# Joining the delta rule's 32-blocks on VectorE, a 64-column last level, and two z tiles moved behind the last heads

## The chip, the cores and the metric

One core of one Trainium2 chip runs one layer of a hybrid decoder block on 256 tokens. The metric is the device time of one execution in microseconds (us). The engines are called as the profile calls them: PE (TensorE, matmuls), PEld (its weight loads), DVE (VectorE), ACT (ScalarE), POOL (GpSimd), SP (SyncE, which only issues DMAs here). ACT and POOL issue DMAs too; such an issue is an instruction in that engine's own queue, between its arithmetic.

## The reference, cut to what matters

The block has two mixers, a Mamba-2 branch and a Gated DeltaNet branch (16 heads, chunks of 64 tokens), then a product-key FFN. The part that the change touches is the inverse in the delta rule:

```python
kk = jnp.einsum('bnhid,bnhjd->bnhij', k, k)
lmat = jnp.where(strict, kk * beta[..., :, None] * decay, 0.0)
t_inv = lax.linalg.triangular_solve(eye + lmat, jnp.broadcast_to(eye, lmat.shape),
                                    left_side=True, lower=True, unit_diagonal=True)
u = t_inv @ (v * beta[..., None])
w = t_inv @ (k * (beta * jnp.exp(gc))[..., None])
```

The kernel uses chunks of 128 tokens, two per head, so each head needs two inverses of unit triangular 128x128 matrices.

## The kernel before, in words

All weights stream from HBM. A **unit** is one weight tile of 512 KB: SP loads it (`raw`), ACT rounds it to its upper part (`whi`, L106), DVE subtracts to get the lower part (`wlo`, L107), and PE runs 12 products of 512 columns on it (L383 to L385, each about a quarter of a microsecond). There are three buffers for the split halves, so when PE starts unit u, ACT can start splitting unit u+2, and units u and u+1 are ready. `schedule()` gives the order of the weight tiles: `qkv` of a head, `gz` (a z gate for two heads), `br gdn j` (the output projection of heads 2j and 2j+1).

Everything else runs as background generators: `bg.step()` is called after every half unit and emits the next step of a generator into the engines' queues when a planner's clock (`Clock`) says that its inputs will be through. The clock takes 0.1 us for a DMA issue on ACT and 4.5 us until it has landed. Once emitted, each engine runs its queue strictly in order. Before `br gdn j` starts, `bg.drain` emits whatever its two heads still lack.

A head (`gdn_gen`) writes its 128x128 matrices `at` to DRAM (`am`, L582). ACT reads the 16 diagonal blocks of 16x16 back, one to a partition (`cu`, L509), POOL inverts them in 30 small steps (L514 to L518) and writes them into `ym` (L522). ACT loads that as `xx` (L590). Then three levels (L592 to L614) join the blocks to 32, 64 and 128 on PE: each has a pair of transposes (L595), a pair of matmuls with the masked or cut `at` (L603, L605) and a pair with the result (L612); ACT and DVE move the results. After that comes the head's chain: `u` (L618, L620), `st` (L629 to L632), `vp` (L637 to L639), the second `u` (L643, L645), `o` (L648 to L661), and `yh`, `yl` (L673 to L676), which the projection reads.

Of the kernel before, what the change touches and what calls it, by code (L numbers as in the profile page):

```python
# [8 lines left out]
F = mybir.dt.float32  # L9
# [3 lines left out]
AF = mybir.ActivationFunctionType  # L13
OP = mybir.AluOpType
# [163 lines left out]
class Background:  # L178
# [61 lines left out]
def block(ctx, tc, nc, I, out, dbg=None):  # L240
    cp = ctx.enter_context(tc.tile_pool(name="consts", bufs=1))
# [3 lines left out]
    dram = ctx.enter_context(tc.tile_pool(name="dram", bufs=1, space=DRAM))  # L245
    V, S, G, PE = nc.vector, nc.scalar, nc.gpsimd, nc.tensor
# [33 lines left out]
    def ps_tile():  # L280
        return psp.tile([128, 512], F, name="pst")
# [6 lines left out]
    cst = cp.tile([128, 5 * 128], F, name="cst")  # L288
# [25 lines left out]
    def tr(dst, src):  # L314
        PE.transpose(dst, src, ident)  # L315
# [170 lines left out]

    corners = [[dram.tile([2, 8, 2064], F, name=n + str(i)) for n in ("am", "ym")] for i in range(2)]

    def whole(m):
        return m.rearrange("c b e -> c (b e)")[:, :128 * 128].rearrange("c (p t) -> p c t", t=128)

    def diagonal(m, i):
        return m[i, :, :2048].rearrange("b (r t) -> b r t", t=128)[:, :, 0:16]

    def clear_corners():
        G.memset(accg[:, 0, :258], 0.0)
        for _, ym in corners:
# [5 lines left out]
    def corner_inverses(am, ym):  # L505

        u, y, tm = (mx.tile([16, 16, 16], F, name=n, bufs=1) for n in ("cu", "cy", "ct"))
        for i in range(2):
            S.dma_start(u[8 * i:8 * i + 8], diagonal(am, i))  # L509
        G.memset(y, 0.0)  # L510
        G.memset(y.rearrange("p a b -> p (a b)")[:, 0:256:17], 1.0)
        yield
        yield pool_free
        for k in range(15, 0, -1):  # L514
            n = 16 - k
            G.tensor_tensor(tm[:, :k, :n], u[:, :k, k:k + 1].to_broadcast([16, k, n]),  # L516
                            y[:, k:k + 1, k:].to_broadcast([16, k, n]), op=OP.mult)
            G.tensor_tensor(y[:, :k, k:], y[:, :k, k:], tm[:, :k, :n], op=OP.subtract)  # L518
            if k in (11, 6):
                yield pool_free  # L520
        for i in range(2):
            G.dma_start(diagonal(ym, i), y[8 * i:8 * i + 8])  # L522
        yield

    def gdn_gen(h, pt, zg, yref):
# [48 lines left out]
        def level(l):  # L574
            b = mx.tile([128, 2, 128], F, name="lev", bufs=3)
            G.tensor_tensor(b, at[:, :, 1, :], masks[:, l - 4:l - 3, :].to_broadcast([128, 2, 128]), op=OP.mult)
            return b

        yield
        live["dT"] -= 1  # L580
        am, ym = corners[h % 2]
        S.dma_start(whole(am), at[:, :, 1, :])  # L582
        yield
        yield lambda: not live["c"] and "at once"
        live["c"] += 1
        yield from corner_inverses(am, ym)
        live["c"] -= 1
        b = level(4)
        xx = mx.tile([128, 2, 2, 128], F, name="xx", bufs=3)
        S.dma_start(xx[:, :, 1, :], whole(ym))  # L590
        yield
        for l in range(4, 7):  # L592
            pm = ps_tile().rearrange("p (a c b) -> p a c b", c=2, a=2)
            for c in range(2):
                tr(pm[:, 0, c, :], xx[:, c, 1, :])  # L595
            S.activation(xx[:, :, 0, :], pm[:, 0], AF.Copy)
            yield
            pm = ps_tile()[:, :256].rearrange("p (c a) -> p c a", c=2)
            m = mx.tile([128, 2, 128], F, name="mm", bufs=3)
            p0 = 64 if l == 6 else 0  # L600
            for c in range(2):
                if l < 6:
                    PE.matmul(pm[:, c, :], b[:, c, :], xx[:, c, 0, :], start=True, stop=True)  # L603
                else:
                    PE.matmul(pm[64:, c, :], at[:64, c, 1, 64:], xx[:64, c, 0, :], start=True, stop=True)  # L605
            S.activation(m[p0:], pm[p0:], AF.Copy)
            if l < 5:
                b = level(l + 1)
            yield
            pb = ps_tile()[:, :256].rearrange("p (c b) -> p c b", c=2)  # L610
            for c in range(2):
                PE.matmul(pb[:, c, :], m[p0:, c, :], xx[p0:, c, 1, :], start=True, stop=True)  # L612
            V.tensor_tensor(xx[:, :, 1, :], xx[:, :, 1, :], pb, op=OP.subtract)
            yield  # L614
        yield lambda: live["u"] < 2
        live["u"] += 1
        pu = ps_tile()
# [45 lines left out]
        if h > 1 and ("gdn", h // 2 - 1) not in merged:  # L663
            yield lambda: ("gdn", h // 2 - 1) in merged
        if h < 2 and not yref:
            mx.tile([128, 32], F, name="pad", bufs=1)
# [124 lines left out]

    small_e = [None, 0, False]
    over, past = set(), set()
    live = {"dT": 0, "u": 0, "c": 0}
    gens, ys, bcT, bcE, gts = {}, {}, {}, {}, {}
    zgs = {("gdn", j): [] for j in range(NH // 2)}

# [78 lines left out]
    for o in order:  # L876
# [20 lines left out]
        if t == ("gz", 0):  # L897
            first.close()
            aux = T16.tile([128, 4, 2, 512], F, name="t16")
            mx = mix.enter_context(tc.tile_pool(name="gdn", bufs=2))  # L900
            masks = mx.tile([128, 3, 128], F, name="masks", bufs=1)
            S.dma_start(masks, I["cst"][:, 1152:].rearrange("p (a b) -> p a b", a=3))
            clear_corners()
        if t == "small":
            evac(ps, 352, raw0)
# [410 lines left out]
```

## Time and profile before

| what | value |
|---|---|
| median of 3 runs | 3427.9 us (3427.09 to 3428.37) |
| the profiled execution | 3427.03 us |
| its span, first to last instruction | 3425.2 us |
| PE busy in the span | 3397.8 us (99%) |
| DVE, ACT, POOL busy | 2233.3, 1755.0, 498.8 us |
| heads of the delta rule | about 50 to 945 us of the span |

The times of the steps come from the profiled execution, so sums are made against its 3427.03 us; the median of the runs is 0.9 us above it. In a timeline each row is the start, the duration and the instruction; PE's matmuls overlap, so what a group of them costs is read from the starts of the products before and behind it.

### The profile page before, as it was taken

What the parts mean: (1) busy time and instruction counts of PE and PEld (TensorE: products, weight loads), DVE (VectorE), ACT (ScalarE), POOL (GpSimd) and SP (SyncE); (2) the same over time, 40 slices, a digit from 0 to 9 for tenths busy, and PEclk for the clock granted to TensorE, in tenths of its full rate; (3) what the DMA queues carried; (4) which work ended last, traced back from release to release, by engine and by line L of the source; (5) the groups of instructions that cost most, each with busy time, mean ns of one, the idle gap of its engine ahead of it and who ended that gap; (6) DMA issues with size and microseconds to landing.
All of it is one profiled execution on the core that took longest, in us unless ns stands there. A gap on an engine that the chain in (4) does not pass through costs nothing.

```text
span 3425.2 us, 43886 instructions
## 1 busy us (share of the span) xinstructions
PE 3397.8 (99%) x16118; PEld 2795.7 (82%) x16118; DVE 2233.3 (65%) x3150; ACT 1755.0 (51%) x2356; POOL 498.8 (15%) x753
## 2 busy tenths in 40 slices
PE   9999999999999999999999999999999999999998
PEld 7888888888888888888888888888888788888886
DVE  6665666676577777777665888766664455555555
ACT  6556555555445454545445445566655444444444
POOL 0434333334200000000000000133230000000000
PEclk9999999999999999999999999999999999999999
DMA  7545555555565555556565566677776877777774
GB/s 258 182 156 158 155 167 157 164 166 156 167 198 177 186 183 186 183 173 200 184 217 191 174 210 210 203 239 231 231 230 223 267 244 241 238 242 244 241 231 162
DMA packets 248408, 687.07 MB, mean 201 GB/s; under 512 B 26736, under 2 KB 86720, under 8 KB 247936
## 3 DMA queue, kind: packets, MB, share of 16 engines
q1 hardware_dynamic: 164960, 594.03, 54.1%
q10 hardware_dynamic: 81824, 87.60, 7.6%
q0 software_dynamic: 1408, 2.64, 0.3%
q8 instruction: 126, 2.06, 0.2%
q14 instruction: 90, 0.74, 0.1%
HBM read 645.81 MB, written 38.36 MB: 200 GB/s over the span
## 4 chain that ended last, share of the span: by engine, by line
PE 96%; DVE 1%; ACT 1%; issue 1%; ACTq 0%; POOL 0%; DMA 0%; POOLq 0%; SPq 0%; DVEq 0%
PE acc L383 23%; PE acc L384 22%; PE acc L385 22%; PE acc L1177 3%; PE acc L1178 3%; PE acc L1183 3%; PE pst L1177 3%; PE pst L1178 3%; PE pst L1183 3%; PE pst L315 3%; PE pst L1104 1%; PE pst L737 1%; PE pst L612 1%; DVE wlo L107 1%; ACT whi L106 0%
## 5 line engine op out<-in xcount | busy, mean ns | idle before, releaser
L107 DVE TENSOR_TENSOR wlo<-raw,whi 128x1024 fp32r<-128x1024 f32 (+1 forms) x1129 | 1419.8, 1266 | 900.5 <-ACT whi L106 898.7
L106 ACT ACTIVATE whi<-raw 128x1024 fp32r<-128x1024 f32 (+1 forms) x1129 | 1184.9, 1052 | 909.6 <-PE acc L385 517.8
L383 PE MATMUL acc<-whi,t 128*128 128x512 f32 (+2 forms) x2848 | 1157.4, 406 | 8.1 <-ACT whi L106 8.1
L384 PE MATMUL acc<-wlo,t 128*128 128x512 f32 (+2 forms) x2848 | 1108.8, 389 | 2.5 <-DVE wlo L107 2.2
L385 PE MATMUL acc<-whi,t 128*128 128x512 f32 (+2 forms) x2848 | 1109.1, 389 | 0.0
L385 PEld LDWEIGHTS acc<-whi,t 128*128 128x128 f32 x2848 | 535.9, 188 | 114.4
L383 PEld LDWEIGHTS acc<-whi,t 128*128 128x128 f32 x2848 | 536.5, 188 | 112.2 <-ACT whi L106 8.6
L384 PEld LDWEIGHTS acc<-wlo,t 128*128 128x128 f32 x2848 | 537.4, 189 | 106.5 <-DVE wlo L107 6.7
L1087 POOL TENSOR_TENSOR b<-ob,gp 128x1024 f16<-128x1024 f16 x64 | 121.5, 1898 | 607.7 <-ACT whi L106 334.0
L383 PE MATMUL acc<-whi,yh 128*128 128x512 f32 x512 | 209.3, 409 | 0.0
L1178 PE MATMUL pst<-wlo,t 128*128 128x512 f32 x512 | 199.9, 391 | 2.1 <-DVE wlo L107 2.1
L384 PE MATMUL acc<-wlo,yh 128*128 128x512 f32 x512 | 200.1, 391 | 0.4 <-DVE wlo L107 0.4
L385 PE MATMUL acc<-whi,yl 128*128 128x512 f32 x512 | 200.0, 391 | 0.0
L1177 PE MATMUL pst<-whi,t 128*128 128x512 f32 x512 | 199.9, 390 | 0.0
L1177 PE MATMUL acc<-whi,t 128*128 128x512 f32 x512 | 199.2, 389 | 0.0
L1178 PE MATMUL acc<-wlo,t 128*128 128x512 f32 x512 | 199.2, 389 | 0.0
L458 DVE SCALAR_TENSOR_TENSOR t<-pst,cols,t 128x255 f32<-128x255 f32 x336 | 135.9, 474 | 33.8 <-ACT t L454 33.7
L1183 PE MATMUL pst<-whi,t 128*128 128x512 f32 x508 | 156.8, 390 | 0.0
L1183 PE MATMUL acc<-whi,t 128*128 128x512 f32 x508 | 156.4, 389 | 0.0
L516 POOL TENSOR_TENSOR ct<-cu,cy 16x15 f32<-16x15 f32 (+7 forms) x240 | 96.8, 403 | 194.4 <-DMA cu<-am 177.0
L1178 PEld LDWEIGHTS pst<-wlo,t 128*128 128x128 f32 x512 | 96.4, 188 | 22.4 <-DVE wlo L107 2.4
L384 PEld LDWEIGHTS acc<-wlo,yh 128*128 128x128 f32 x512 | 96.3, 188 | 21.3 <-DVE wlo L107 1.3
(273 smaller groups left out, 3286.8 us busy)
## 6 DMA issues: line engine op xcount, KB each, us to landing
raw<-w_in SPq DMA_DIRECT2D x408, 512.0 KB
raw<-u SPq DMA_DIRECT2D x256, 512.0 KB
raw<-v SPq DMA_DIRECT2D x256, 512.0 KB
raw<-w_gdn SPq DMA_DIRECT2D x64, 512.0 KB
raw<-w_ssm SPq DMA_DIRECT2D x64, 512.0 KB
raw<-w_out SPq DMA_DIRECT2D x32, 512.0 KB
raw<-w_q SPq DMA_DIRECT2D x32, 512.0 KB
hdr<-ht ACTq DMA_DIRECT2D x32, 512.0 KB
```

The lines of the kernel that those rows point to most:

```text
L106: self.nc.scalar.activation(hi[:, s], t[:, s], AF.Copy)
L107: self.nc.vector.tensor_tensor(lo[:, s], t[:, s], hi[:, s].bitcast(F), op=OP.subtract)
L315: PE.transpose(dst, src, ident)
L383: PE.matmul(o, xa, h_, start=k == 0, stop=False)
L384: PE.matmul(o, xa, l_, start=False, stop=False)
L385: PE.matmul(o, xb, h_, start=False, stop=k == nk - 1)
L458: V.scalar_tensor_tensor(dst[:, s:], src[:, :T - s], w[:, c, k:k + 1], dst[:, s:], op0=OP.mult, op1=OP.add)
L516: G.tensor_tensor(tm[:, :k, :n], u[:, :k, k:k + 1].to_broadcast([16, k, n]), y[:, k:k + 1, k:].to_broadcast([16, k, n]), op=OP.mult)
L1087: G.tensor_tensor(b2, ob[:, None, :, :].to_broadcast([128, 2, 4, 128]), gp[:, :, ts, None].to_broadcast([128, 2, 4, 128]), op=OP.mult)
L1177: PE.matmul(o_, a, hi[:, s], start=i2 == 0, stop=False)
L1178: PE.matmul(o_, a, lo[:, s], start=False, stop=False)
L1183: PE.matmul(acc[tb][2 * hv + n], b, hi[:, n * 512:(n + 1) * 512], start=False, stop=False)
```

## The change

Per head, the join from 16 to 32 leaves PE. POOL also writes the 16x16 inverses and their transposes to a new DRAM tile `yb`. When that is done, ACT issues 18 DMAs in one step: 8 loads of the blocks beside the diagonal, broadcast so that each of 128 partitions holds one block and one column (`cb`, 64-byte rows), 8 of the second inverse (`c1`) and 2 of a column of the first (`c2`). DVE then multiplies and sums twice (128x256 each), and ACT writes the 16x16 results into `ym` with 2 DMAs. The join to 64 stays on PE (now from the transposed blocks), and the join to 128 uses 64x64 transposes and matmuls of 64 rows and 64 columns. There are 12 PE instructions per head in place of 18, and 25 DMA issues on ACT in place of 5. The corner buffers go from 2 to 3, the planner's backlog from 2.5 to 3.0, and z tile 6 moves from behind `br gdn 3` to behind `br gdn 5`, next to z tile 7, so that `br gdn 4` and `br gdn 5` each come one tile earlier.

```diff
-        if j != 6:
-            o.append(("in", ("gz", min(j + 1, 7))))
+        o += [("in", ("gz", i)) for i in ((1,), (2,), (3,), (4,), (5,), (), (), (6, 7))[j]]
...
-    def __init__(self, clock, backlog=2.5):
+    def __init__(self, clock, backlog=3.0):
...
+    def beside(m, i, below):
+
+        rows = m[i].rearrange("b e -> (b e)").rearrange("(j f) -> j f", j=4)[:, 2048 * below:2048 * below + 2048]
+        o = 0 if below else 16
+        return rows.rearrange("j (r t) -> j r t", t=128)[:, :, o:o + 16]
...
+        G.tensor_copy(tm, y.rearrange("p a b -> p b a"))
+        G.dma_start(yb[0].rearrange("c b e -> (c b) e"), y.rearrange("p a b -> p (a b)"))
+        G.dma_start(yb[1].rearrange("c b e -> (c b) e"), tm.rearrange("p a b -> p (a b)"))
         for i in range(2):
-            G.dma_start(diagonal(ym, i), y[8 * i:8 * i + 8])
+            G.dma_start(diagonal(ym, i), tm[8 * i:8 * i + 8])
+        live["c"] -= 1
+        yield
+        yield lambda: not live["d"] and "at once"
+        live["d"] += 1
...
+        for i in range(2):
+            for j in range(4):
+                S.dma_start(bb[64 * i + 16 * j:64 * i + 16 * j + 16],
+                            beside(am, i, 0)[j:j + 1].to_broadcast([16, 16, 16]))
+        for i in range(2):
+            for j in range(4):
+                p = slice(64 * i + 16 * j, 64 * i + 16 * j + 16)
+                S.dma_start(y1[p], yb[0, i, 2 * j:2 * j + 1].to_broadcast([16, 256]))
+            S.dma_start(y2[64 * i:64 * i + 64, 0, :],
+                        yb[1, i].rearrange("(j b) (q r) -> j b q r", b=2, q=16)[:, 1])
+        yield
+        V.scalar_tensor_tensor(pr, bb, -1.0, y2[:, 0:1, :].to_broadcast([128, 16, 16]), op0=OP.mult, op1=OP.mult)
+        V.tensor_reduce(y2[:, 1, :], pr, axis=mybir.AxisListType.X, op=OP.add)
+        V.tensor_tensor(pr, y1, y2[:, 1:2, :].to_broadcast([128, 16, 16]), op=OP.mult)
+        V.tensor_reduce(y2[:, 2, :], pr, axis=mybir.AxisListType.X, op=OP.add)
+        live["d"] -= 1
+        yield
+        for i in range(2):
+            S.dma_start(beside(ym, i, 1), y2[64 * i:64 * i + 64, 2, :])
...
+        for c in range(2):
+            PE.matmul(pm[:, c, :], b[:, c, :], xx[:, c, 0, :], start=True, stop=True)
+        for c in range(2):
+            tr(pb[:, c, :], xx[:, c, 0, :])
...
+        lo, hi = slice(0, 64), slice(64, 128)
+        pm = ps_tile()[:, :128].rearrange("p (c a) -> p c a", c=2)
+        for c in range(2):
+            PE.transpose(pm[lo, c, :], xx[lo, c, 1, lo], ident[lo, lo])
+        S.activation(xx[lo, :, 0, lo], pm[lo], AF.Copy)
+        yield
+        pm = ps_tile()[:, :128].rearrange("p (c a) -> p c a", c=2)
+        for c in range(2):
+            PE.matmul(pm[hi, c, :], at[lo, c, 1, hi], xx[lo, c, 0, lo], start=True, stop=True)
...
+            PE.matmul(pb[lo, c, :], m[hi, c, lo], xx[hi, c, 1, hi], start=True, stop=True)
```

Two places show what moves. The first is ACT's queue in the fifth head's chain (`u`, `st`, `o`, second `u`), before:

```order
L620 ACTIVATE u_3457<-pst,cc 128x256
L535 DMA dT<-racs 128x256
L632 ACTIVATE st<-pst 128x256
L634 ACTIVATE junk,so<-pst 128x256
L790 ACTIVATE t_3478<-acc,r_111 128x512 x2
L106 ACTIVATE whi<-raw 128x1024
L640 ACTIVATE o<-pst,ecs 128x256
L546 ACTIVATE junk,w_3512<-pst 128x128 x4
```

In the changed kernel, the same head's chain with the next head's 18 loads in it (`cb`, `c_3770` and `c_3772` are the tiles they fill; lines are those of the changed kernel):

```order
L661 ACTIVATE u_3743<-pst,cc 128x256
L105 ACTIVATE whi<-raw 128x1024
L545 DMA cb<-am_143 16x16x16 x8
L550 DMA c_3770<-yb_145 16x256 x4
L551 DMA c_3772<-yb_145 64x1x16
L550 DMA c_3770<-yb_145 16x256 x4
L551 DMA c_3772<-yb_145 64x1x16
L607 ACTIVATE vp<-pst,nk 128x256 x2
L105 ACTIVATE whi<-raw 128x1024
L673 ACTIVATE st<-pst 128x256
```

The same burst from its eighth DMA on, with the semaphores that each waits for. ACT's and SP's DMAs signal eight semaphores in turn (DMAHW0 to DMAHW7), so each waits for the last DMA that had its own:

```order
L545 DMA cb<-am_143 16x16x16 [waits DMAHW7_49]
L550 DMA c_3770<-yb_145 16x256 [waits DMAHW0_49,DMASW7_49]
L550 DMA c_3770<-yb_145 16x256 [waits DMAHW1_49]
L550 DMA c_3770<-yb_145 16x256 [waits DMAHW2_49]
L550 DMA c_3770<-yb_145 16x256 [waits DMAHW3_49]
L551 DMA c_3772<-yb_145 64x1x16 [waits DMAHW4_49,DMASW0_49]
L550 DMA c_3770<-yb_145 16x256 [waits DMAHW5_49]
L550 DMA c_3770<-yb_145 16x256 [waits DMAHW6_49]
L550 DMA c_3770<-yb_145 16x256 [waits DMAHW7_49]
L550 DMA c_3770<-yb_145 16x256 [waits DMAHW0_49]
L551 DMA c_3772<-yb_145 64x1x16 [waits DMAHW1_49]
```

So between `u` and `st` ACT has 18 DMA issues where it had one. The second place is PE's queue where `br gdn 5` begins (its products read `yh`), before:

```order
L383 MATMUL acc<-whi,t_105 128x512
L384 MATMUL acc<-wlo,t_105 128x512
L385 MATMUL acc<-whi,t_106 128x512
L612 MATMUL pst<-xx,mm 128x128 x2
L383 MATMUL acc<-whi,yh 128x512
```

And now (L684 and L689 are the second `u` and `o` of head 11, L314 on `o` the transposes that `yh` is made from):

```order
L384 MATMUL acc<-whi,t_106 128x512
L604 MATMUL pst<-cT 128x256 x2
L684 MATMUL pst<-vp,xx 128x256
L689 MATMUL pst<-u_7296,at 128x256
L314 MATMUL pst<-cst,t_6991 128x128 x4
L314 MATMUL pst<-cst,o 128x128 x4
L382 MATMUL acc<-whi,yh 128x512
```

The end of head 11's chain, which ran among the products of the tile before, now stands directly ahead of the projection, with no products between its steps.

## Rows read from the trace of the kernel before

**Rows 1.** Page, part 1: busy us, share of span, instructions of each engine.

```profile
PE 3397.8 (99%) x16118; PEld 2795.7 (82%) x16118; DVE 2233.3 (65%) x3150; ACT 1755.0 (51%) x2356; POOL 498.8 (15%) x753
```

**Rows 2.** Windows: length, PE, PEld, DVE, ACT, POOL busy, PE's clock, DMA share, GB/s.

```profile
250.00:350.00 100.00, 99.66 (x484) 81.51 (x483) 60.62 (x100) 61.27 (x117) 45.81 (x94) 1.00 0.51 159
```

**Rows 3.** Timeline of PE, one head's levels: start, duration, instruction.

```profile
403.55 0.61 PE L612 MATMUL pst<-xx,mm 128*128 128x128 f32 x4
...
404.23 0.39 PE L384 MATMUL acc<-wlo,t 128*128 128x512 f32 x1
...
405.39 0.38 PE L315 MATMUL pst<-cst,xx 128*128 128x128 f32 x2
405.61 0.60 PE L315 MATMUL pst<-cst,t 128*128 128x128 f32 x4
...
407.20 0.40 PE L385 MATMUL acc<-whi,t 128*128 128x512 f32 x1
407.53 0.65 PE L605 MATMUL pst<-xx,at 64*64 64x128 f32 x4
...
408.44 0.40 PE L384 MATMUL acc<-wlo,t 128*128 128x512 f32 x1
...
409.39 0.39 PE L385 MATMUL acc<-whi,t 128*128 128x512 f32 x1
409.70 0.71 PE L612 MATMUL pst<-xx,mm 64*128 64x128 f32 x4
...
410.68 0.40 PE L384 MATMUL acc<-wlo,t 128*128 128x512 f32 x1
```

**Rows 4.** Timeline of PE in the Mamba-2 branch, matmuls of 64 columns.

```profile
1025.62 1.89 PE L737 MATMUL pst<-xdt,sc 128*128 128x64 f32 x16
```

**Rows 5.** DMA issues by tile: issue time min/median/max in ns; last, landing of POOL's.

```profile
L509 ACTq DMA_DIRECT2D cu<-am x32: 288/332/535, 111.6 to 863.0; - x32
L590 ACTq DMA_DIRECT2D xx<-ym x16: 371/387/388, 143.9 to 894.5; - x16
DMA to landing us min/median/max: 1.9/3.3/5.2
```

**Rows 6.** Timeline of ACT late in the FFN: four DMA issues in a row (ACTq).

```profile
2683.33 1.06 ACT L106 ACTIVATE whi<-raw 128x1024 fp32r<-128x1024 f32 x1 [1.66 <-PE acc L385]
...
2686.06 2.99 ACTq L1139 DMA_DIRECT2D m<-gdr  x2
2689.07 3.85 ACTq L1143 DMA_DIRECT2D p<-hdr  x2
2693.03 1.06 ACT L106 ACTIVATE whi<-raw 128x1024 fp32r<-128x1024 f32 x1 [6.29 <-DMA m<-gdr]
```

**Rows 7.** Timeline of PE over the same stretch.

```profile
2691.78 0.39 PE L384 MATMUL acc<-wlo,t 128*128 128x512 f32 x1
2692.01 0.40 PE L385 MATMUL acc<-whi,t 128*128 128x512 f32 x1
2694.14 0.51 PE L383 MATMUL acc<-whi,t 128*128 128x512 f32 x1 [1.73 <-ACT whi L106]
2695.40 0.79 PE L384 MATMUL acc<-wlo,t 128*128 128x512 f32 x1 [0.75 <-DVE wlo L107]
...
2698.54 0.39 PE L385 MATMUL acc<-whi,t 128*128 128x512 f32 x1
```

**Rows 8.** Windows, just behind that: columns as in rows 2.

```profile
2695.10:2698.50 3.40, 3.10 (x7) 2.48 (x8) 2.40 (x3) 1.96 (x3) 0.00 (x0) 0.50 1.07 385
```

**Rows 9.** Timeline of ACT at the last head's end: second u, then yh.

```profile
933.37 0.48 ACT L645 ACTIVATE u<-pst,cc 128x256 f32<-128x256 f32 x1
...
942.45 0.48 ACT L330 ACTIVATE yh<-pst,cols 128x256 fp32r<-128x256 f32 x1 [0.74 <-PE pst L315]
```

**Rows 10.** Groups by line: count, busy us, mean ns of one, idle us before.

```profile
L613 DVE TENSOR_TENSOR xx<-xx,pst 128x256 f32<-128x256 f32 x48 | 19.9, 415 | 14.7 <-PE pst L612 14.7
L576 POOL TENSOR_TENSOR lev<-at,masks 128x256 f32<-128x256 f32 x32 | 35.9, 1129 | 0.0
```

More of the change, by code (lines that the diff above doesn't have):

```diff
@@ L485, in input_tile @@
         return mx.tile([128, 2, 512], F, name="t4", bufs=NT4[0])
-    corners = [[dram.tile([2, 8, 2064], F, name=n + str(i)) for n in ("am", "ym")] for i in range(2)]
+    corners = [(dram.tile([2, 8, 2064], F, name="am%d" % i), dram.tile([2, 8, 2064], F, name="ym%d" % i),
+                dram.tile([2, 2, 8, 256], F, name="yb%d" % i)) for i in range(3)]
     def whole(m):
@@ L503, in pool_free, with corner_inverses @@
         return "at once" if bg.clock.t["Pool"] < bg.clock.t["PE"] + 2.0 else False
-    def corner_inverses(am, ym):
+    def corner_inverses(am, ym, yb):
+        yield lambda: not live["c"] and "at once"
+        live["c"] += 1
         u, y, tm = (mx.tile([16, 16, 16], F, name=n, bufs=1) for n in ("cu", "cy", "ct"))
@@ L520, in corner_inverses @@
                 yield pool_free
+        G.tensor_copy(tm, y.rearrange("p a b -> p b a"))
+        G.dma_start(yb[0].rearrange("c b e -> (c b) e"), y.rearrange("p a b -> p (a b)"))
+        G.dma_start(yb[1].rearrange("c b e -> (c b) e"), tm.rearrange("p a b -> p (a b)"))
         for i in range(2):
-            G.dma_start(diagonal(ym, i), y[8 * i:8 * i + 8])
+            G.dma_start(diagonal(ym, i), tm[8 * i:8 * i + 8])
[3 more added lines that the diff above has]
+        live["d"] += 1
+        bb, y1, pr = (mx.tile([128, 16, 16], F, name=n, bufs=1) for n in ("cb", "c1", "cp"))
+        y2 = mx.tile([128, 3, 16], F, name="c2", bufs=2)
+        for i in range(2):
[17 more added lines that the diff above has]
+            S.dma_start(beside(ym, i, 1), y2[64 * i:64 * i + 64, 2, :])
         yield
@@ L572, in gdn_gen @@
             V.tensor_scalar(at[:, c, 1, :], at[:, c, 1, :], cc[:, c:c + 1], None, op0=OP.mult)
[L574 to L577, printed above, removed]
         yield
         live["dT"] -= 1
-        am, ym = corners[h % 2]
+        am, ym, yb = corners[h % 3]
         S.dma_start(whole(am), at[:, :, 1, :])
         yield
-        yield lambda: not live["c"] and "at once"
@@ L585, in gdn_gen @@
[L585 to L588, printed above, removed]
+        yield from corner_inverses(am, ym, yb)
         xx = mx.tile([128, 2, 2, 128], F, name="xx", bufs=3)
-        S.dma_start(xx[:, :, 1, :], whole(ym))
+        S.dma_start(xx[:, :, 0, :], whole(ym))
+        b = mx.tile([128, 2, 128], F, name="lev", bufs=2)
+        G.tensor_tensor(b, at[:, :, 1, :], mask[:, None, :].to_broadcast([128, 2, 128]), op=OP.mult)
         yield
[L592 to L614, printed above, removed]
@@ new lines, in gdn_gen @@
+        pm = ps_tile()[:, :256].rearrange("p (c a) -> p c a", c=2)
+        pb = ps_tile()[:, :256].rearrange("p (c a) -> p c a", c=2)
+        for c in range(2):
+            PE.matmul(pm[:, c, :], b[:, c, :], xx[:, c, 0, :], start=True, stop=True)
+        for c in range(2):
+            tr(pb[:, c, :], xx[:, c, 0, :])
+        m = mx.tile([128, 2, 128], F, name="mm", bufs=3)
+        S.activation(m, pm, AF.Copy)
+        V.tensor_copy(xx[:, :, 1, :], pb)
+        yield
+        pb = ps_tile()[:, :256].rearrange("p (c b) -> p c b", c=2)
@@ new lines, in gdn_gen @@
+        for c in range(2):
+            PE.matmul(pb[:, c, :], m[:, c, :], xx[:, c, 1, :], start=True, stop=True)
+        V.tensor_tensor(xx[:, :, 1, :], xx[:, :, 1, :], pb, op=OP.subtract)
+        yield
+        lo, hi = slice(0, 64), slice(64, 128)
[3 more added lines that the diff above has]
+        S.activation(xx[lo, :, 0, lo], pm[lo], AF.Copy)
+        yield
+        pm = ps_tile()[:, :128].rearrange("p (c a) -> p c a", c=2)
@@ new lines, in gdn_gen @@
+        for c in range(2):
+            PE.matmul(pm[hi, c, :], at[lo, c, 1, hi], xx[lo, c, 0, lo], start=True, stop=True)
+        m = mx.tile([128, 2, 128], F, name="mm", bufs=3)
+        S.activation(m[hi, :, lo], pm[hi], AF.Copy)
+        yield
+        pb = ps_tile()[:, :128].rearrange("p (c b) -> p c b", c=2)
+        for c in range(2):
+            PE.matmul(pb[lo, c, :], m[hi, c, lo], xx[hi, c, 1, hi], start=True, stop=True)
+        V.tensor_tensor(xx[lo, :, 1, hi], xx[lo, :, 1, hi], pb[lo], op=OP.subtract)
@@ L615, in gdn_gen @@
+        yield
         yield lambda: live["u"] < 2
@@ L665, in gdn_gen @@
         if h < 2 and not yref:
-            mx.tile([128, 32], F, name="pad", bufs=1)
+            mx.tile([128, 64], F, name="pad", bufs=1)
         if not yref:
@@ L900, in block @@
             mx = mix.enter_context(tc.tile_pool(name="gdn", bufs=2))
-            masks = mx.tile([128, 3, 128], F, name="masks", bufs=1)
-            S.dma_start(masks, I["cst"][:, 1152:].rearrange("p (a b) -> p a b", a=3))
+            live["d"] = 0
+            mask = mx.tile([128, 128], F, name="mask", bufs=1)
+            S.dma_start(mask, I["cst"][:, 1280:1408])
             clear_corners()
```

4 lines of the change are left out of this document (2 added, 2 removed).

## The prediction

> **What bounds the kernel now.** I read the page's busy line first: PE is busy 3397.8 of 3425.2 us [rows 1], so the time is the sum of PE's own instructions plus every moment in which PE is made to wait. Then the windows, to see whether the heads' stage is different: in 250 to 350 us PE is busy 99.66 of 100 us while DVE has 60.62, ACT 61.27 and POOL 45.81 [rows 2]. So each matmul that leaves PE is a gain in full, and work added to the others is free on the mean. The mean hides one thing: ACT feeds PE a split weight tile every unit, and PE has only two units ready when it begins one. So I then looked for a place where ACT's queue holds something long, and found one in the FFN [rows 6 to 8].
>
> The sum is made against the profiled run's 3427.0 us (span 3425.2 and 1.8 around it); the median of the runs is 3427.9, so 0.9 is added at the end.
>
> **What leaves PE.** What a group costs is read from the starts around it, less 0.23 us for each undisturbed product (2691.78 to 2692.01) [rows 7]. A pair of transposes: 405.39 to 405.61, 0.22. A pair of full matmuls: 403.55 to 404.23 holds the pair and one product, 0.68 - 0.23 = 0.45. The 64-row pairs are dearer: 407.20 to 408.44 holds two products and the pair, 1.24 - 0.46 = 0.78, and 409.39 to 410.68 gives 0.83 [rows 3]. The join to 32 is 0.22 + 0.45 + 0.45 = 1.12 us a head and goes: 16 x 1.12 = 18. The join to 64 keeps its six.
>
> The join to 128 is 0.22 + 0.78 + 0.83 = 1.83 now; no row shows its new form (64 rows and 64 columns). Sixteen passes of 64 columns took 1.89, 0.118 each [rows 4], and a pass of 128 columns costs 0.45 / 4 = 0.11 [rows 3], so by the nearest row half the columns save nothing. If time did follow columns, each matmul pair would save 0.22. The transposes become a 64-row group: 0.22 if that costs nothing, 0.22 + 0.33 if it pays what a 64-row pair pays over a full one (0.78 - 0.45). So the level lies between 1.39 and 2.16, a gain of 7 to a loss of 5 us over 16 heads; I take 0, by rows 4. PE's own work falls by 18 us (13 to 25).
>
> The Trainium skill, TensorEngine Tiling (Array Packing), section Key Properties, says that changing the tiling mode drains TensorE; the trace's 0.33 us over a full pair agrees with that, and the rule speaks against the third 64-row group. By that rule alone the sum would be some 5 us worse than mine.
>
> **What DVE and POOL get.** DVE has four new operations of 128x256 and a copy, and loses one subtract and most of another: at 0.415 us each [rows 10] about 1.7 us a head net. POOL loses one mask product of 1.13 [rows 10] and gets a copy and two DMA issues, about as much. Both are covered by the 39 and 54 idle us in 100 [rows 2], so I cost them at nothing; were DVE's cover gone, 16 x 1.7 = 27 us. DVE's first new operation also waits for the last of the loads, and `wlo` is queued behind it. The planner puts it 6.5 us behind the burst's start, the loads land later (below), but PE and the `wlo` ahead of it are late by the same cause by then, so this wait lies under that one and is not added. The two issues into `ym` and the load of `xx` wait as `am`, `cu` and `xx` did before.
>
> **What ACT gets: 18 DMA issues in a row, 16 times.** ACT loses three short activations a head, but its queue now holds a burst of 18 issues. One takes 0.33 us (L509) to 0.39 (L590) [rows 5], so the burst lasts 6.0 to 7.0 us by issue alone. With eight semaphores the eighth waits for the landing of the first, each later one for one some seven or eight ahead of it, and three or four for SP's loads. Landings are 1.9 / 3.3 / 5.2 us (min/median/max) for POOL's DMAs, the nearest row [rows 5]. With 3.3 the eighth goes at 3.3 behind the first, the sixteenth at 6.3, the seventeenth at 7.0, and the burst ends at 7.7; with 1.9 it is bound by issue, 7.0; with 5.2 it ends at 11.5. I take 7.7. The planner books 18 x 0.1 = 1.8 us, so what it emits behind the burst comes some 6 us too early.
>
> Queued behind it on ACT are the next `whi`, the previous head's `st`, second `u` or `o`, and `vp`; DVE waits for that `whi`, and PE for both and for the second `u` (L648 before, L689 now). A walk through the burst that is emitted behind unit 106, with t = 0 where PE starts that unit: the activation ahead of the burst starts at 0, so the issues run from 0 to 7.7; then `whi` for unit 108 (1.06) to 8.8, then the second `u` (0.48) at 9.3. PE reaches the matmul that needs it after one unit (12 x 0.23 = 2.75), one pair (0.45) and half a unit (1.38): 4.6. PE waits 4.7 us. Where no such matmul is near, as behind unit 61, the next `whi` decides: the burst starts 1.2 behind the start of unit 60 and ends at 8.9, the write of `am` takes 0.39, `whi` ends at 10.4 and `wlo` 1.26 later (2694.14 to 2695.40 [rows 7]) at 11.6; PE has three units and a pair, 9.1, and waits 2.5. In the same way the 15 bursts that lie among products give 2.3 to 4.7, 3.8 on the mean; all move one for one with the burst's length.
>
> The trace of before has one such case. Four issues held ACT from 2686.06 to 2693.03, 6.9 us, 2.7 behind a `whi` [rows 6]. PE then waited 1.73 and 0.75 us, and the granted clock behind it was 0.50, the 1.2 GHz level, for 3.4 us [rows 8]. From 2692.01 to 2698.54 PE made nine starts, which are 2.07 us of products: that burst cost 4.5 us [rows 7]. I take 4.5 for each of the 15, between 2.1 (burst of 6.0, full clock) and 5.5 (7.7, and each wait followed by 3.4 us at the half clock, worth 1.7): 67 us.
>
> **The sixteenth burst and the moved z tile.** With z tile 6 gone from there, `br gdn 5` follows head 11's input sooner, and the drain ahead of it emits the burst, the second `u` and the rest of the chain with no product between. From second `u` to `yh` took 9.1 us at the last head [rows 9]. Ahead of the second `u` stand what is left of the burst (7.7 less the 1.1 that it began before the tile's end, 6.6), and four activations, two for `vp` and two that evacuate the next head's input: 1.9 at 0.48 each (256 columns, rows 9), at most 4.2 at 1.06 (1024 columns, rows 6). With 1.9 the chain ends at 17.6; the transposes of `o`, behind which PE goes on, come 0.7 ahead of `yh`. PE fills 2.7 of it with its own groups (by rows 3, a matmul of 256 columns counted as two of 128, 4 x 0.45, and eight transposes, 4 x 0.22): 14 us of waiting, 11 to 18. The tiles themselves only change places.
>
> **Sum.** 3427.0 - 18 + 67 + 14 = 3490, and 0.9 for the median: **3491 us**.
>
> **Rivals.** *The bursts are hidden.* PE's two ready units would cover them if a burst were no longer than 7.7 - 3.8 = 3.9 us, 0.22 for an issue; then only the 18 us remain: 3427.9 - 18 = 3410 (3403 to 3415), faster. For it: ACT is idle 39 of 100 us. Against it: no issue of the 48 in rows 5 is under 0.288, and the four in rows 6 did hold ACT. I give it 0.09. The Trainium skill, DMA: Bandwidth & Descriptors, section Issuing engines are not separate DMA queues, calls the time to initiate a DMA on the sequencer usually small relative to the DMA, and Anatomy of one DMA puts the sequencer's dispatch at some 50 ns; by that a burst would be an estimated 0.9 us and this rival would hold, but the rows show six times as much.
>
> *The change does its work and gives it back.* Bursts of 6.0 with early landings and clocks that stay full would cost 2.1 each at most; were half of them covered too, 15 x 1.0 + 11 - 25 is near nothing: 3428 (within 0.2%, which is about what a measurement of this kernel can tell from no change). 0.05.
>
> *Issue alone counts.* Bursts of 6.0 and full clock everywhere: -18 + 31 + 11: 3452 (3436 to 3465). 0.17.
>
> *Landings count.* 64-byte rows landing as late as 5.2 make bursts of 11.5 and waits of 7.6, 9.3 with the half clock: -18 + 139 + 18: 3567. 0.09. Forecast: 0.60, with 3465 to 3535 for itself.
>
> **How the numbers follow.** Faster 0.09, same 0.05, slower 0.86. The range leaves out the two cases below (0.14) and most of the last: 3436 to 3535.
>
> **What would show it.** Right: ACT idle before `whi` of 6 to 8 us sixteen times with ACTq rows of L545 to L551 beside it; PE waiting 2 to 5 us at L689 or at the first product of a unit, each followed by a stretch at 0.50; one wait of about 14 us ahead of `br gdn 5`; PE's busy time at full clock down by some 18. The 64-row groups' starts show the last level. Wrong: ACTq issues well under 0.3 us, or `whi` starting between them, or PE at 99% in the windows of the heads' stage as before.

## The result: 3548.5 us, 3.5% slower than before

The changed kernel takes 3548.5 us (median of 4 runs, 3547.3 to 3550.1) against 3427.6 for the kernel before on the same chip: a ratio of 1.035 (95% interval 1.034 to 1.037). The direction and the mechanism were forecast, the size was not: +121 us in place of +63, above the range's end of 3535.

The page of the changed kernel, part 1, answers to [rows 1]. PE is busy 96% of a span that is 121 us longer:

```profile
PE 3411.1 (96%) x15958; PEld 2795.7 (79%) x15958; DVE 2256.2 (64%) x3214; ACT 1731.9 (49%) x2308; POOL 524.3 (15%) x786
```

The window of [rows 2], now: PE loses 12 of 100 us, and its mean clock falls to 0.93.

```profile
250.00:350.00 100.00, 87.26 (x395) 70.17 (x395) 58.98 (x101) 52.09 (x99) 47.32 (x84) 0.93 0.49 145
```

What PE waits for (waits of PE over the whole span: engine and line, releaser, us in total, times, longest). ACT's `u` and `whi` and what hangs on them stand first (`u` is the input of the chain's `o` step at L689, `whi` a split weight tile):

```profile
PE pst L689 <- ACT u L686: 53.6, 8, 10.9
PE acc L382 <- ACT whi L105: 29.2, 7, 6.6
PE pst L684 <- DVE vp L680: 15.7, 5, 7.5
PE pst L314 <- POOL o L702: 10.3, 3, 6.4
```

One burst, on ACT (timeline: start, duration, instruction; in brackets idle time and its releaser). From 366.25 to 375.14 ACT's queue gives out nothing but DMAs (the activation `o`, begun just before, ends at 366.72), and `u` stands behind them:

```profile
366.24 0.48 ACT L681 ACTIVATE o<-pst,ecs 128x256 f32<-128x256 f32 x1 [1.39 <-DVE vp L680]
366.25 3.81 ACTq L545 DMA_DIRECT2D cb<-am  x8
370.16 1.82 ACTq L550 DMA_DIRECT2D c<-yb  x4
372.07 0.56 ACTq L551 DMA_DIRECT2D c<-yb  x1
372.67 1.88 ACTq L550 DMA_DIRECT2D c<-yb  x4
374.59 0.55 ACTq L551 DMA_DIRECT2D c<-yb  x1
375.19 1.06 ACT L105 ACTIVATE whi<-raw 128x1024 fp32r<-128x1024 f32 x1 [8.47 <-DMA c<-yb]
...
376.15 0.46 ACT L686 ACTIVATE u<-pst,cc 128x256 f32<-128x256 f32 x1
```

The same burst on PE. It stops for 6.39 us at L689, which needs that `u`, and then starts products every 0.43 us in place of 0.23:

```profile
369.88 0.39 PE L384 MATMUL acc<-whi,t 128*128 128x512 f32 x1
376.66 1.22 PE L689 MATMUL pst<-u,at 128*128 128x256 f32 x2 [6.39 <-ACT u L686]
377.32 0.99 PE L382 MATMUL acc<-whi,t 128*128 128x512 f32 x1
378.11 0.63 PE L383 MATMUL acc<-wlo,t 128*128 128x512 f32 x1
378.54 0.63 PE L384 MATMUL acc<-whi,t 128*128 128x512 f32 x1
```

Windows of that stretch (columns as in rows 2): the granted clock is 0.50, the 1.2 GHz level, from 372.5, while PE stands idle, up to 382.7; in the last 6.3 us of that PE works:

```profile
376.40:382.70 6.30, 6.04 (x14) 4.80 (x15) 3.95 (x5) 3.52 (x7) 1.17 (x3) 0.50 0.60 178
372.50:376.30 3.80, 0.00 (x0) 0.00 (x0) 0.02 (x1) 1.11 (x2) 0.00 (x0) 0.50 0.12 31
```

The sum of it, from the trace between 110 and 1110 us: PE's gaps over 0.1 us come to 109.8 us (3.2 before), of which 14.9 lie in the drain ahead of `br gdn 5`; work done at the half clock comes to 77.3 us and so cost 38.7 (0 before). PE's own work fell by 16 x 1.40 = 22.4 (1.14 for the join to 32, 0.26 for the last level; see the part on the prediction). 106.6 + 38.7 - 22.4 = 122.9, and the span grew by 121.2. Outside the drain that is 15 bursts (a burst is one row of 18 issues) at about 6.1 us of waiting and 2.3 of half clock: 8.4 each, where the prediction had 4.5.

### The profile page after: what moved, and what is told of

It reads as the page before. It is cut to its first block, busy times and chain, and to the rows that moved or that the text cites. A ratio compares the mean times of both kernels' runs of the same rounds, so it can differ in the third digit from the quotient of the medians.

```text
span 3546.4 us, 44055 instructions
## 1 busy us (share of the span) xinstructions
PE 3411.1 (96%) x15958; PEld 2795.7 (79%) x15958; DVE 2256.2 (64%) x3214; ACT 1731.9 (49%) x2308; POOL 524.3 (15%) x786
## 4 chain that ended last, share of the span: by engine, by line
PE 89%; ACT 2%; DVE 2%; ACTq 2%; DMA 2%; issue 1%; POOL 0%; POOLq 0%; SPq 0%; DVEq 0%
PE acc L382 21%; PE acc L383 21%; PE acc L384 21%; PE acc L1220 3%; PE acc L1219 3%; PE acc L1225 3%; PE pst L1225 3%; PE pst L1219 3%; PE pst L1220 3%; PE pst L314 3%; ACTq L550 1%; DVE wlo L106 1%; ACT whi L105 1%; DMA raw<-w_in 1%; PE pst L1146 1%
## 5 line engine op out<-in xcount | busy, mean ns | idle before, releaser
L106 DVE TENSOR_TENSOR wlo<-raw,whi 128x1024 fp32r<-128x1024 f32 (+1 forms) x1129 | 1424.5, 1270 | 960.9 <-ACT whi L105 957.3
L527 POOL TENSOR_TENSOR ct<-cu,cy 16x15 f32<-16x15 f32 (+7 forms) x240 | 115.4, 481 | 108.4 <-DMA cu<-am 91.4
L382 PEld LDWEIGHTS acc<-whi,yh 128*128 128x128 f32 x512 | 98.0, 191 | 31.0 <-ACT whi L105 8.6
```

The lines of the kernel that those rows point to most:

```text
L106: self.nc.vector.tensor_tensor(lo[:, s], t[:, s], hi[:, s].bitcast(F), op=OP.subtract)
L382: PE.matmul(o, xa, h_, start=k == 0, stop=False)
```

## Experiments

The theory after the result, called the queue theory in the expectations: ACT's queue is held by a row of DMA issues, and PE runs out of split tiles or stops at a matmul that needs an activation behind the row. Its rivals are the order of the z tiles, the late data, and the planner's price. "Idle" and "half clock" below are worked out as in the sum above, between 110 and 1110 us.

**1. The burst alone, in the kernel before.**

```diff
+        for i in range(2):
+            for j in range(4):
+                S.dma_start(bb[...], <8 blocks of am, broadcast>)
+        for i in range(2):
+            for j in range(4):
+                S.dma_start(y1[p], <rows of am, broadcast>)
+            S.dma_start(y2[...], <rows of am>)
```

> The kernel before with 18 loads of the same shapes added per head at the place where the change has them (from am alone); nothing reads them, PE, DVE and POOL have the work of before. Queue theory: 16 bursts of about 10 us, each some 6.1 us of idle PE and 2.3 of half clock: 3427.9 + 134 = 3562 (3530 to 3590). Rival (data theory: PE waits because the joined blocks come late and the head's chain with them): nobody waits for these loads, so 3428 to 3440.

3579.9 us, 1.045 (1.043 to 1.047): 153 us more, for loads that nobody reads. PE's waits (columns as above; this kernel's L106, L661 and L664 are `whi`, `u` and its matmul):

```profile
PE acc L383 <- ACT whi L106: 50.5, 11, 6.3
PE pst L664 <- ACT u L661: 29.4, 7, 8.6
```

Idle 103.9, half clock 45.7; the bursts last 10.0 us on the mean, as in the changed kernel. The burst by itself is the whole price, and late data is out. It is some more than in the changed kernel, as PE's saving isn't in it: 153 - 22 = 131, near 121. The nearer comparison is the changed kernel with the z tiles in the order that this run has (experiment 8): it takes 133 us more than the kernel before.

**2. All but the burst, in the changed kernel.**

```diff
-        (the 18 loads, the four DVE operations, the two writes into ym)
+        (z tiles in the order of before)
```

> As the run before, but the join to 32 is left out: no 18 loads, no four DVE operations, no write of their result (the output is not the reference's); POOL still writes the inverses, the joins to 64 and 128 stay. Queue theory: no burst, no waiting, and only PE's own saving is left: by the changed kernel's trace the join to 32 was 1.14 us a head and the last level fell by 0.26, so 3427.9 - 16 x 1.40 = 3405. Rival (planner's backlog of 3.0, POOL's additional DMAs, or 64-row groups cost the time): well above 3428.

3407.6 us, 0.9945 (0.9928 to 0.9961): 19.2 less than before, with 4.9 us of idle PE and no half clock. So backlog, POOL's additional DMAs and the new levels cost nothing that shows. This kernel leaves out the join to 32 altogether, so 19 us is what the change would give if that join were free.

**3. Fewer issues: ten, and four.** In the first the eight loads of `c1` become one DMA, and the two of `c2` one. In the second the blocks beside the diagonal are packed by one DMA in DRAM, so that `cb` is one load too; of its four issues three stand in a row.

```diff
+        S.dma_start(y1, yb[0].rearrange("c (j b) e -> (c j) b e", b=2)[:, 0:1, :].to_broadcast([8, 16, 256]))
+        S.dma_start(y2[:, 0, :], yb[1].rearrange("c (j b) (q r) -> (c j) b q r", b=2, q=16)[:, 1])
```

```diff
+        all_beside = am.rearrange("c b e -> (c b e)").rearrange("(j f) -> j f", j=8)[:, :2048]
+        S.dma_start(ab.rearrange("j (r t) -> j r t", t=16), all_beside.rearrange("j (r t) -> j r t", t=128)[:, :, 16:32])
...
+        S.dma_start(bb.rearrange("p a b -> p (a b)"), ab[:, None, :].to_broadcast([8, 16, 256]))
```

> The changed kernel with the eight loads of c1 as one DMA and the two of c2 as one: 10 issues in place of 18, the same bytes and rows. Queue theory with a fixed price per issue (0.49 us from one start to the next): bursts of 5.4 us, PE's idle per burst 5.4 - 3.8 = 1.6 in place of 6.1, half clock 1 in place of 2.3: 3548 - 16 x 5.8 = 3455 (3440 to 3475). Rival (an issue's time goes with the rows it describes, so the one DMA takes as long as the eight): 3548. Rival (data theory): 3548 less a few us.

> The changed kernel with one DMA from DRAM to DRAM that packs the blocks beside the diagonal (behind the loads of cu), one for cb, one for c1, one for c2: 4 issues in place of 18, three of them in a row. Queue theory: a burst of three takes 1.5 to 2 us by issue, 4 with one wait for a landing: 3407.6 + 5 to 25 = 3413 to 3433. Rival (waits for landings set a burst's length, not the number of issues; ten issues took 7.0 us of which 1.8 were such waits): three issues would still last 4 to 5 and cost 1 to 2 us each with the half clock: 3430 to 3450. Rival (data theory): the joined blocks come as late as before, 3548.

Ten: 3506.4 us, 1.023 (1.021 to 1.025); the bursts last 7.0 us on the mean, of which 1.8 are waits for landings, not the 5.4 expected, and only 42 us came back. Four: 3418.4 us, 0.9974 (0.9964 to 0.9984), **9 us less than the kernel before and 130 less than the changed kernel**. PE is back at 99%, and the three issues hold ACT for 1.9 us (page part 1, then ACT's timeline in head 11's chain):

```profile
PE 3373.6 (99%) x15958; PEld 2772.3 (81%) x15958; DVE 2258.7 (66%) x3214; ACT 1735.1 (51%) x2308; POOL 518.7 (15%) x786
```

```profile
728.07 0.63 ACTq L546 DMA_DIRECT2D cb<-ab  x1
728.75 0.61 ACTq L547 DMA_DIRECT2D c<-yb  x1
729.40 0.58 ACTq L548 DMA_DIRECT2D c<-yb  x1
730.10 1.06 ACT L105 ACTIVATE whi<-raw 128x1024 fp32r<-128x1024 f32 x1 [1.95 <-PE pst L680]
```

An issue of eight times the rows takes 0.6 us in place of 0.43, so here the price is by the DMA far more than by the row.

**4. Half the burst, in the kernel before.**

```diff
+        for dst, src in loads[::2]:
+            S.dma_start(dst, src)
```

> As the run with 18 additional loads in the kernel before (3580), but with every second of them: 9 issues in a row per head; nothing reads them. Queue theory with cover (PE has some 3.8 us ready, what is longer costs its length and a half clock behind it): bursts of 4.4 by issue and 1 to 1.5 for landings, 5.7 together, so 1.9 of idle and about 1 of half clock a head: 3427.9 + 46 = 3474 (3455 to 3490). Rival (no cover: each issue costs its time): half of the 153 of the run with 18, 3504. Rival (only landings count): as with 18, 3560 or more.

3507.9 us, 1.024 (1.023 to 1.026): 83 more, which is the rival's figure (half of 153) and not 46. But 23 of it lie in one drain at the last head, whose chain comes later with the additional step (13.7 of idle, 9.6 of half clock; 13 in the run with 18). What is left is 60 here and some 140 there, 3.7 and 8.8 a burst. The bursts last 5.0 us, and outside the drains idle is 37.6, 34 or 2.1 a burst more than before; with bursts of 10.0 it is 91.9, 89 or 5.5 a burst. So there is a cover, of 3 to 4.5 us, but it is no fixed one: 5.0 us more of burst brought 3.4 more of waiting.

**5. The same loads in threes.** First in the changed kernel:

```diff
+        for n, (dst, src) in enumerate(loads):
+            S.dma_start(dst, src)
+            if n % 3 == 2 and n < 17:
+                yield 0
```

> The changed kernel with the same 18 loads on ACT, but three to a step of the planner, so that a half unit of products (1.38 us of PE) and ACT's other work stand between one group and the next. Queue theory (it is the length of one uninterrupted burst, 10.0 us on the mean, against the 3.8 that PE has ready): a group takes 1.5 us, 3 to 4 with one wait for a landing, so nearly no wait is left outside the drain: 3407.6 (the kernel without the loads) + 5 to 25 = 3413 to 3433. Rival (ACT's total time counts, 18 x 0.49 us a head however they are spread): 3548. Rival (data theory, the loads come later still): 3548 or more.

3520.8 us, 1.027 (1.026 to 1.029). The edit did less than I wrote: the planner runs up to two steps at every half unit, so groups of three to nine issues as a rule, and twice all 18, still stand between one `whi` and the next. And 48 of the 82.9 us of idle are four drains now: the head's chain is later, and its end stands ahead of a projection with no products between. In PE's waits `o` on POOL, the last step of a chain, comes first:

```profile
PE pst L314 <- POOL o L704: 26.6, 8, 11.8
```

Then in the kernel before, in a generator of its own, with a plain `yield`, so that the planner waits 4.5 us between the threes:

> The kernel before with the 18 additional loads, nothing reads them, but from a generator of their own, three at a time, and the next three only when the planner's clock has the last three landed (4.5 us), so that whi and the chain's steps come between on ACT's queue. Queue theory: a group of three takes 1.5 us, up to 4 with a landing, which PE's ready units cover: 3428 to 3442. Rival (ACT's total time counts, or what the 288 small DMAs do to the transfers of the weights): as in a row, 3580, or at least 3500.

3478.9 us, 1.015 (1.014 to 1.017). The groups are threes for the most part now, of 1.4 us (median). 100 of the 153 us are gone, so holding the queue in one piece is the larger part. The 53 that stay were not expected. Idle is 36.1 and half clock 12.5: 9.9 of idle in the last head's drain, the rest in waits of up to 4.7 us, for `yh`, `xx`, `wlo`, `vp` and `u` above all; some 7 of the 53 are in neither sum. What of it is ACT's 18 x 0.45 us, what is steps that the planner gives away to the loads, and what the additional DMAs do to other transfers stays open.

**6. The planner told the price.**

```diff
-            self.t[e] = start + 0.1
+            self.t[e] = start + (0.5 if e == "Activation" else 0.1)
```

> The changed kernel with the planner told 0.5 us for a DMA issue on ACT in place of 0.1; the 18 loads stay one burst. Planner theory (the waits are those of a chain step emitted too early behind a burst that was booked at 1.8 us; 9 of the 16 long waits in the changed kernel's trace name an activation of the chain): the planner holds these steps back, PE waits for whi alone, some 4 us a burst: 3548 - 9 x 3 = 3520 (3500 to 3530). Queue theory in its plain form (two units ready, a burst of 10): no more than 10 come back, 3538 to 3548. If the price were the whole cause: 3430.

3591.5 us, 1.048 (1.046 to 1.050): 43 slower, not 28 faster. The waits did change their names as expected: for `u` 8.2 us are left of 53.6, and there are 13 waits for `whi` of 4.7 us on the mean, which is the idle that a burst brings when nothing of the chain is near.

```profile
PE acc L382 <- ACT whi L105: 61.5, 13, 6.7
PE pst L314 <- POOL o L702: 24.2, 4, 11.9
```

But a planner that holds the chain back until ACT has caught up finishes it late, and 59.1 us of idle stand in four drains (14.9 in one in the changed kernel). So a planner that books the price does not take the burst out of the queue, and the price is not the whole cause.

**7. The loads on other queues.** `G.dma_start` (POOL) and `nc.sync.dma_start` (SP) in place of `S.dma_start` for the 18 loads, in a row.

> The changed kernel with the 18 loads issued from POOL's queue in place of ACT's. Queue theory: ACT is as free as in the kernel before, so PE's waits of the bursts vanish: 3407.6 + 5 to 30 for the drain and for a later chain = 3413 to 3438. Rival (data theory: DVE's new operations wait for the last load and wlo stands behind them): the waits stay, 3500 or more, since POOL starts its DMAs one by one as well. Rival (POOL becomes late: a DMA issue holds it 1 us or more, and its 30 steps for the next head wait): drains late, 3440 to 3480.

3472.8 us, 1.013 (1.012 to 1.015): the last rival's range. ACT's part is gone: PE waits 2.4 us for `u`, and `whi` is no longer among its waits of note. But an issue holds POOL for 0.49 to 0.56 us, 9.4 for 18, and `o`, the last step of a chain, runs on POOL: PE waits 34.0 us for it, six times. In the three longest, 6.9 to 8.4 us, `o` stands directly behind the row (end of one row on POOL):

```profile
247.68 3.31 POOL L552 DMA_DIRECT2D c<-yb  x6 [0.34 <-issue]
251.01 1.27 POOL L702 TENSOR_TENSOR o<-o,t 128x512 f32<-128x512 f32 x1
```

> The changed kernel with the 18 loads in a row on SP's queue in place of ACT's; SP otherwise only loads the weight tiles. Queue theory (it is ACT being held): SP has some 3 tiles loaded or under way ahead of the split and PE two split ones, so 9 us of SP's queue are covered for the most part: 3407.6 (no loads at all) + 5 to 25 for the drain and a late tile now and then = 3413 to 3433. Rival (the small DMAs hold the weight loads wherever they are issued, or their landings hold DVE's wlo): 3470 to 3548. Rival (SP's loads come late in place of ACT's splits): PE waits for whi with ACT waiting for raw, 3450 to 3520.

3594.6 us, 1.049 (1.047 to 1.051), the slowest of all. SP's queue is in order too, and the weight loads in it (L94) wait for their buffer to be read by DVE, so the 18 loads stand behind them and come late. DVE's first new operation waits for the last of them, and `wlo` is queued behind it (waits of SP, of DVE, then of PE):

```profile
SPq L94 <- DVE wlo L106: 611.1, 197, 13.0
```

```profile
DVE cp L554 <- DMA c<-yb: 171.0, 16, 13.1
```

```profile
PE acc L383 <- DVE wlo L106: 100.2, 16, 10.7
```

So the late data that the first experiment ruled out for ACT's queue does decide on SP's. Even the three loads in a row of the version with the fewest issues (3418.0, the second run of experiment 9) cost there; the pack in DRAM stays on ACT:

> The kernel of the fewest issues (3418.0) with its loads of cb, c1 and c2 on SP in place of ACT, so that ACT has as many issues a head as the kernel before, two of them dearer. Queue theory: the few short waits that are left in the heads' stage outside the last drain (8 us) shrink: 3410 to 3416. Rival (what is left is PE's own work and the drain of the last heads): 3418. If SP must wait for POOL's writes with weight loads behind it: 3425 to 3440.

3479.9 us, 1.016 (1.014 to 1.017), 62 more than the same loads on ACT, with DVE waiting 73.3 us for them.

**8. The z tiles.** The changed kernel, and the one with four loads, with z tile 6 behind `br gdn 3` as before.

```diff
-        o += [("in", ("gz", i)) for i in ((1,), (2,), (3,), (4,), (5,), (), (), (6, 7))[j]]
+        if j != 6:
+            o.append(("in", ("gz", min(j + 1, 7))))
```

> The changed kernel with the z tiles in the order of before (z tile 6 behind br gdn 3); all else as changed. In the changed kernel's trace the drain ahead of br gdn 5 has PE idle 10.9 + 3.7 = 14.6 us and a stretch of 20.5 us at the half clock. Queue theory (each burst of 18 DMA issues on ACT costs PE its length less what PE has ready): the sixteenth burst then lies among products like the other fifteen, some 6 us of idle and 2 of half clock in place of 14.6 and about 7, so 3548 - 13 = 3535. Rival (z order): the move of the tiles takes cover from more heads than one, and 30 us or more come back: 3518 or less. Rival (order without a price): 3548.

> The kernel with four loads (3418.4) with the z tiles in the order of before. The drain ahead of br gdn 5, where it has PE idle for 4.5 us, is covered again (-5), and the last heads have one tile less behind them: with bursts the same edit added 10.4 us of idle and 23.9 us at the half clock there in place of nothing. So 3418.4 - 5 + 10 to 20 = 3423 to 3433. Rival (the prediction's: the tiles only change places, and the drain ahead of br gdn 5 is the one price): 3413.

3559.4 us, 11 slower than the changed kernel, and 3424.8, 6.4 slower than with four loads. The drain ahead of `br gdn 5` does go, but another comes at the last heads, where a tile is missing. In the first of the two kernels the end of head 15's chain stands bare on PE from the join to 64 on (L628; L315 on `o` is the last step):

```profile
1050.61 0.39 PE L385 MATMUL acc<-whi,t 128*128 128x512 f32 x1
1052.88 0.68 PE L628 MATMUL pst<-xx,lev 128*128 128x128 f32 x4 [1.87 <-DMA xx<-ym]
...
1073.51 1.11 PE L315 MATMUL pst<-cst,o 128*128 128x128 f32 x4 [4.57 <-POOL o L703]
1074.28 0.77 PE L383 MATMUL acc<-whi,yh 128*128 128x512 f32 x1
```

It takes 23.7 us from product to product, 11.4 of them idle, the rest mostly at 0.50. The cause is the head's longer path, not the bursts alone, since the version with four loads has the drain too (22.2 us from product to product, 10.2 of them idle). From the `cu` loads of the last head to its `xx` the kernel before took 863.0 to 894.5, 31.5 us [rows 5]. The changed kernel takes 66, with a burst and PE's stops in it, and the version with four loads, where a row takes 1.9 us, takes 48 (two tiles' issue rows for each: duration min/median/max in ns, first and last start; the changed kernel, then four loads):

```profile
L520 ACTq DMA_DIRECT2D cu<-am x32: 283/330/539, 109.6 to 963.1; - x32
```

```profile
L620 ACTq DMA_DIRECT2D xx<-ym x16: 377/387/392, 167.1 to 1029.2; - x16
```

```profile
L521 ACTq DMA_DIRECT2D cu<-am x32: 287/331/600, 110.0 to 847.3; - x32
```

```profile
L616 ACTq DMA_DIRECT2D xx<-ym x16: 366/387/392, 158.4 to 895.3; - x16
```

**9. The last level, and the fewest issues.** The version with four loads with the last level of before; and with z tile 6 ahead of `br gdn 5`, `cu` in one load and the joined blocks in one write.

> The kernel with four loads (3418.4) with the last level of before: 128x128 transposes, matmuls of 64 rows and 128 columns. By the starts in the changed kernel's trace the new level costs 0.43 + 0.58 + 0.57 = 1.58 us a head, the old one 1.83 in the kernel before, so 16 x 0.26 = 4 us come back: 3422 (3420 to 3426). Rival (the term of the prediction, half the columns save nothing): 3418.

> The kernel with four loads, with z tile 6 ahead of br gdn 5 in place of behind it, one load in place of two for cu, and one DMA in place of two for the joined blocks into ym. The drain ahead of br gdn 5 (4.5 us of idle PE with four loads) is covered by a tile of products, the last heads keep as many tiles behind them, and ACT has two issues less a head: 3418.4 - 4 to 8 = 3410 to 3414. Rival (what is late there is late again one tile on): 3418.

3424.9 us, 0.9995 (0.9986 to 1.0004), 6.5 more. The profiled executions are 8.0 us apart; 5.0 of that are more idle and half clock among the heads and about 1 in the FFN. What is left, some 2 us, has the sign of the 4 us from the trace but doesn't prove them. The other: 3418.0, 0.9977 (0.9968 to 0.9986), no different from 3418.4. The drain ahead of `br gdn 5` went (1.6 us of idle), but the one at the last heads grew by as much, from 7.2 to 8.8: near the rival's reading, with the delay coming back further on.

## Why the prediction was right in kind and wrong in size

**The limit and the mechanism: right.** PE at 99% made every wait count, ACT's queue was the place, and the waits stand at L689, L684 and at the first product of a unit for the most part, each followed by a stretch at 0.50, as forecast; but they are 3.6 to 8.0 us long, not 2 to 5. "Bursts are hidden" and "gives it back" fell with experiment 1. The bursts' length came out between the forecast's 7.7 and the 11.5 of "landings count".

**The failed step: "One takes 0.33 us (L509) to 0.39 (L590) [rows 5], so the burst lasts 6.0 to 7.0 us by issue alone."** Those were issues that stood alone or in pairs, and a row was never priced. In a row they cost more: in the changed kernel (issue rows as above)

```profile
L545 ACTq DMA_DIRECT2D cb<-am x128: 310/460/1157, 140.1 to 1006.3; - x128
```

```profile
L550 ACTq DMA_DIRECT2D c<-yb x128: 309/431/547, 144.2 to 1011.6; - x128
L551 ACTq DMA_DIRECT2D c<-yb x32: 540/557/635, 148.2 to 1012.1; - x32
```

The first of a row takes 0.31 to 0.33, each directly behind another 0.43 to 0.47 as a rule (the two of 64 rows 0.55), with 0.04 between them: 8.9 us is the shortest burst. The trace of the kernel before held such a price, in a row of the profile that I did not use: of the loads of `p`, which ACT issues two at a time, the first takes 0.33 and the second 0.45.

```profile
L967 ACTq DMA_DIRECT2D p<-x x8: 334/392/451, 1754.3 to 1823.4; - x8
```

Waits for semaphores then add 1.0 us on the mean (0 to 3.2), where I had added 0.7 to 1.7 to a burst limited by landings. The mean burst is 10.0 us, not 7.7. The 2.3 us more explain the wait: 3.8 + 2.3 = 6.1 was measured. But experiment 4 shows 3.4 us of wait for 5.0 of burst and not one for one, so that the match to a tenth is in part luck.

**The half clock: under-sized.** I took the FFN's case as a whole, 4.5 with 1.7 of half clock in it [rows 8], although my own walk through the bursts gave 3.8 of waiting, 5.5 with that half clock: 1.0 us a burst was lost there. The longer waits bring 6.8 us at 0.50 as a rule, and the work in it costs 2.3 a burst, 0.6 more than 1.7. With the 2.3 of the longer burst that makes the 3.9 between 4.5 and 8.4: the term is 15 x 8.4 = 126 and not 67. That is the whole miss of 57, as the two other terms were off by 4 and 5 us in opposite directions.

**The drain ahead of `br gdn 5`: nearly right for itself, wrong as the price of the edit.** 14 us was forecast, 11 to 18; 10.93 and 3.72 are there, in the steps named, plus 7.4 us of work at the half clock (3.7 us), 18.6 in all:

```profile
834.42 0.67 PE L684 MATMUL pst<-vp,xx 128*128 128x256 f32 x2 [0.20 <-DVE vp L680]
846.02 1.22 PE L689 MATMUL pst<-u,at 128*128 128x256 f32 x2 [10.93 <-ACT u L686]
...
851.82 1.12 PE L314 MATMUL pst<-cst,o 128*128 128x128 f32 x4 [3.72 <-POOL o L702]
852.59 0.78 PE L382 MATMUL acc<-whi,yh 128*128 128x512 f32 x1
```

But "The tiles themselves only change places" failed: experiment 8 shows that the move gains 11 us in the changed kernel and 6 with four loads, because the head's path is longer (48 us in place of 31.5 with four loads, 66 with bursts) and the last heads need the tile behind them. The prediction put a head's longer path at nothing.

**PE's own work: 22 less, within 13 to 25.** (22 is worked out from starts; experiment 2, without the join, came out 19 us faster.) For the last level I took the wrong row. The starts (one undisturbed stretch, products dropped) give 234.11 to 235.15, 1.04 - 0.46 = 0.58, and 1.02 - 0.46 = 0.56:

```profile
234.11 0.40 PE L384 MATMUL acc<-whi,t 128*128 128x512 f32 x1
234.44 0.44 PE L647 MATMUL pst<-xx,at 64*64 64x64 f32 x4
...
235.15 0.40 PE L383 MATMUL acc<-wlo,t 128*128 128x512 f32 x1
...
236.08 0.39 PE L384 MATMUL acc<-whi,t 128*128 128x512 f32 x1
236.40 0.44 PE L653 MATMUL pst<-xx,mm 64*64 64x64 f32 x4
...
237.10 0.39 PE L383 MATMUL acc<-wlo,t 128*128 128x512 f32 x1
```

So half the columns saved 0.20 to 0.27 of each pair [rows 3], against rows 4, and the 64-row transposes cost 0.43 in place of 0.22 (medians over 13 to 15 heads: 0.43, 0.58, 0.57; 1.58 in place of 1.83). Why 64 columns saved nothing in rows 4 and something here stays open. The join to 32 measured 1.14 where 1.12 was forecast. The Trainium skill, TensorEngine Tiling (Array Packing), section Key Properties, says that changing the tiling mode drains TensorE. The trace agrees: the third 64-row group costs 0.20 us a head more than the full one that it replaces, though the level as a whole became cheaper.

**DVE: covered, as forecast.** DVE has no wait for the loads at all in the changed kernel; experiment 7 shows that this was true of ACT's queue only (14.4 us of waiting with POOL's, 171.0 with SP's). POOL, put at about no change, is busy 1.6 us a head longer (524.3 for 498.8).

**The rival with an issue of 50 ns.** The Trainium skill, DMA: Bandwidth & Descriptors, section Anatomy of one DMA, gives the sequencer's dispatch as some 50 ns, by which a row of 18 would take an estimated 0.9 us. It says so of DMAs issued from GpSimd, which the prediction did not notice when it carried the figure over to ACT. The traces have more on both engines: 8.9 us at the least for ACT's row, 0.49 to 0.56 for one issue on POOL (experiment 7).

## What to carry to other kernels

Price DMA issues from issues that stand in a row, and count them by the DMA: 18 small loads on a compute engine are a 9 us hole in its queue, and merging them to four turned a loss of 121 us into a gain of 9. Before moving them to another queue, ask what that queue's head waits for and which engine waits for the data: POOL had the chain's last step behind them, SP had blocked weight loads ahead of them. When a background chain gets longer, look at its end: what was hidden behind products becomes a drain where the consumer comes next.

## What was not expected of the hardware

- Of the 18 loads, an issue directly behind another on ACT took 0.43 to 0.47 us as a rule (a few up to 1.16), the first of a row 0.31 to 0.33, the two of 64 rows 0.54 to 0.64. In the version with four loads, those of 128 rows took 0.58 to 0.63 (once 0.72). It is no fixed price: the second of a pair of `cu` loads took 0.33 in the changed kernel. What of a DMA sets it no run here singles out. On POOL an issue held the engine for 0.49 to 0.56.
- The granted clock fell to 0.50 while PE stood idle (in 15 of the 16 stretches among the heads of the changed kernel; once 1.1 us behind a wait), and stayed there 3.4 to 10.2 us (20.5 in the drain). Part of that time was idle anyway: of some 126 us at 0.50 in the heads' stage of the changed kernel only 77.3 had work in them. The FFN's stop of rows 7, 2.5 us of idle, was followed by 3.4 us at 0.50; in the changed kernel it came again, with 2.7 us of idle, and no such stretch followed.
